# Row normalisation of 1024 x 4096: both stores issued by GpSimd, and the last scale of the first tile on VectorE alone

## The chip, the cores and the metric

The kernel runs on one core of a Trainium2 chip. Four of its engines matter here: VectorE and ScalarE compute, Sync and GpSimd issue transfers. The bytes are moved by 16 DMA engines, which take their work from queues; a transfer goes into the queue of the engine that issued it. The time is device microseconds of one execution; a figure quoted is a median of several. All runs here were in the fast state: the granted clock was 1.0 everywhere, and the executions of most kernels agree within 0.3%. "Span" is the time from the first to the last instruction in the trace; the timed figure is some 1.8 us longer for every kernel here, so what changes in the time is inside the span. One execution of each kernel was profiled, so each figure below that comes from a trace is of one execution.

## The reference

```python
batch, dim = 1024, 4096                       # x: float32
norm = np.sqrt(np.sum(x ** 2, axis=-1, keepdims=True) + eps)
return x / norm
```

So 16.78 MB are read and 16.78 MB are written, and each element is touched twice in between: once to square it, once to scale it.

## The kernel before

The 1024 rows are two tiles of 128 partitions x 4 rows x 4096. Both loads are issued at once by Sync. Each tile is squared (three rows on ScalarE, one on VectorE), scaled in place on VectorE, and stored in one transfer of 8.39 MB. Each tile has a buffer of its own, so no load waits for a store.

The lines on which the change rests, shortened (the whole kernel follows below):

```python
def scale(self, r):                            # VectorE, whole row
    nc.vector.tensor_scalar_mul(out=x[:, r], in0=x[:, r], scalar1=rstd[:, r:r+1])

def scale_by_both(self, r):                    # 7/8 on ScalarE, 1/8 on VectorE
    cut = 7 * D // 8
    nc.scalar.activation(out=x[:, r, :cut], in_=x[:, r, :cut], func=Copy, scale=rstd)
    nc.vector.tensor_scalar_mul(out=x[:, r, cut:], in0=x[:, r, cut:], scalar1=rstd)

for i, g in enumerate(groups):
    ...                                        # squares, norms, scales of rows 0, 1, 3
    g.square_act(2); g.norm(2)
    if i < n_tiles - 1:
        g.scale_by_both(2)                     # last scale of the first tile
    else:
        g.scale(2)
    store = nc.sync.dma_start(out=out_t[i], in_=g.flat())
gpsimd_waits_for_last_store(nc, store.ins)
```

The last line rewrites the program's teardown. That consists of two barriers of all engines (points at which each waits for the others), with drains ahead of them. A drain is an instruction at which an engine waits for its own earlier work: VectorE's took 2.39 us in the kernel before, beside its last scale of 2.35 us. Before the rewriting Sync waits for the last store. The rewriting lets only GpSimd wait for it, at the last step of the second barrier, so that everything else of both barriers happens while store 2 still moves.

## Time and profile before

| | before |
|---|---|
| median | 81.8 us |
| span of the profiled execution | 80.2 us |
| 16 DMA engines busy | 97.4% of the span |
| store 1 issued, load 2's data ends | 38.99 us; 40.27 to 41.05 us on the 16 engines |
| store 2 issued, store 1's data ends | 56.76 us; 59.79 to 60.37 us |
| last packet ends, span ends | 79.69 us, 80.20 us |

The busy share and the times of issue come from the views that the prediction shows. The ends of packets come from the records of single DMA packets in the trace: a packet here is one partition's 64 KiB, each of the 16 engines moves 32 of them one after the other, and nearly all take 2.418 us. To read a joint of two transfers one can take a stretch of the trace around it and divide busy time by bytes. In the stretch from 40.2 to 45.0 us, that is where load 2 gives way to store 1, the kernel before has (columns: stretch, length, busy DVE, ACT, POOL, clock, DMA share, GB/s):

```profile
40.20:45.00 4.80, 3.60 (x1) 3.60 (x2) 0.00 (x0) 1.00 1.01 437
79.70:80.20 0.50, 0.00 (x0) 0.00 (x0) 0.00 (x0) 1.00 0.00 0
```

437 GB/s for 4.8 us are 2.1 MB, two packets on each of the 16 engines, and a share of 1.01 says that the two together took 1.01 x 4.8 = 4.85 us, 2.42 us each. A share well over 1 in such a row means that packets which started in the stretch took longer than their usual time, if the stretch cuts no packets (a row in part 5 has 1.08 for that reason alone); so the readings below are checked against the packet records. Nor does a share of 1 rule out idle time: by the records, 5 of the 16 engines stood idle for 0.19 to 0.24 us between load 2 and store 1 here. They weren't the last to end, so it cost nothing. The second row is the tail after the last packet.

### The profile page before, as it was taken

Reading aid. Unit: us, or ns where it says so; the run is one execution under the profiler, and the core shown is the slowest. Engines: PE = TensorE matmul, PEld = TensorE weight load, DVE = VectorE, ACT = ScalarE, POOL = GpSimd, SP = SyncE. Lnnn points to the kernel's source line nnn. Section 1 sums busy time; section 2 is a strip of 40 time slices with the busy share of each in tenths; the row PEclk is TensorE's granted clock in tenths of the full one; section 3 lists DMA queues with packets and bytes.
Section 4 is the critical chain, followed back from the end, with each engine's and each line's share of the span. In section 5 each row is a group of like instructions: output and inputs, shape, how many; then the busy total and the mean of one; then the engine's idle time right before and its main releaser. Section 6 shows DMA issues by size and latency. Waiting matters only on the chain.

```text
span 80.2 us, 93 instructions
## 1 busy us (share of the span) xinstructions
DVE 26.7 (33%) x21; ACT 29.7 (37%) x23; POOL 0.2 (0%) x4
## 2 busy tenths in 40 slices
DVE  0000000000099599960039995999200000000000
ACT  6000000000099999989439999950000000000000
POOL 0000000000000000000000000000000000000000
DMA  9099996699996699996699990999991999992990
GB/s 490 33 523 523 523 490 294 261 523 523 523 490 261 294 523 523 523 490 261 294 523 523 523 490 33 523 523 523 523 458 65 523 523 523 523 425 98 523 523 0
DMA packets 576, 33.55 MB, mean 418 GB/s; under 512 B 64, under 2 KB 64, under 8 KB 64
## 3 DMA queue, kind: packets, MB, share of 16 engines
q1 hardware_dynamic: 576, 33.55, 97.4%
HBM read 16.78 MB, written 16.78 MB: 418 GB/s over the span
## 4 chain that ended last, share of the span: by engine, by line
DMA 51%; ACT 10%; DVE 9%; issue 0%
DMA xt<-in_x_dram 51%; ACT sq_act L33 9%; DVE xt L64 9%; ACT rstd L53 1%; DVE rstd L59 0%
## 5 line engine op out<-in xcount | busy, mean ns | idle before, releaser
L33 ACT ACTIVATE sq_act<-xt 128x4096 f32<-128x4096 f32 x6 | 21.7, 3609 | 22.4 <-DMA xt<-in_x_dram 22.4
L42 DVE SCALAR_TENSOR_TENSOR sq_dve<-xt 128x4096 f32<-128x4096 f32 x2 | 8.9, 4426 | 26.4 <-DMA xt<-in_x_dram 26.4
L64 DVE TENSOR_SCALAR xt<-xt,rstd 128x4096 f32<-128x4096 f32 x7 | 16.5, 2353 | 0.2
L72 ACT ACTIVATE xt<-xt,rstd 128x3584 f32<-128x3584 f32 x1 | 3.3, 3283 | 0.2 <-DVE rstd L59 0.2
L53 ACT ACTIVATE rstd<-ssq,eps_t 128x1 f32<-128x1 f32 x8 | 2.1, 290 | 0.1
L59 DVE RECIPROCAL rstd<-rstd 128x1 f32<-128x1 f32 x8 | 1.3, 160 | 2.5 <-ACT rstd L53 2.5
L33 ACT ACT_TABLE_LOAD x1 | 1.3, 1283 | 0.8 <-PEq L258 0.8
L53 ACT ACT_TABLE_LOAD x1 | 1.3, 1283 | 0.0
L33 ACT ACTIVATION_READ_ACCUMULATOR sq_act<-xt 128x1 f32 x6 | 1.1, 187 | 0.0
L78 DVE TENSOR_SCALAR xt<-xt,rstd 128x512 f32<-128x512 f32 x1 | 0.5, 487 | 0.0
L211 DVE MEMSET eps_t<- 128x1 f32 x1 | 0.1, 59 | 0.9 <-PEq L258 0.9
L42 DVE DVE_READ_ACCUMULATOR sq_dve<-xt 128x1 f32 x2 | 0.2, 83 | 0.0
L258 POOL MEMSET const-uint8-127<- 128x1 uint8 x1 | 0.1, 103 | 0.0
L258 POOL MEMSET const-bfloat16-1.0<- 128x1 bf16 x1 | 0.1, 102 | 0.0
L258 POOL MEMSET const-float32-0.0<- 128x1 f32 x1 | 0.1, 99 | 0.2 <-issue 0.2
L258 POOL MEMSET const-float32-1.0<- 128x1 f32 x1 | 0.1, 99 | 0.0
## 6 DMA issues: line engine op xcount, KB each, us to landing
xt<-in_x_dram SPq DMA_DIRECT2D x2, 31.3
out_dram<-xt SPq DMA_DIRECT2D x2, 22.5
```

The source lines that it names most:

```text
L33: self.nc.scalar.activation(out=sq_a, in_=self.x[:, r], func=ACT_F.Square, accum_out=self.ssq[:, r : r + 1],)
L42: self.nc.vector.scalar_tensor_tensor(out=sq_v, in0=self.x[:, r], scalar=1.0, in1=self.x[:, r], op0=ALU.mult, op1=ALU.mult, accum_out=self ...
L53: self.nc.scalar.activation(out=self.rstd[:, r : r + n], in_=self.ssq[:, r : r + n], func=ACT_F.Sqrt, bias=self.eps_t,)
L59: self.nc.vector.reciprocal(out=self.rstd[:, r : r + n], in_=self.rstd[:, r : r + n])
L64: self.nc.vector.tensor_scalar_mul(out=self.x[:, r], in0=self.x[:, r], scalar1=self.rstd[:, r : r + 1])
L72: self.nc.scalar.activation(out=self.x[:, r, :cut], in_=self.x[:, r, :cut], func=ACT_F.Copy, scale=rstd,)
L78: self.nc.vector.tensor_scalar_mul(out=self.x[:, r, cut:], in0=self.x[:, r, cut:], scalar1=rstd)
L211: nc.vector.memset(eps_t, eps)
L258: nc = _bacc.Bacc("TRN2", target_bir_lowering=False, num_devices=1)
```

## The change

Its intent, as far as the diff tells: GpSimd, idle until the end, takes the stores from Sync, and the first tile's last scale becomes shorter (one VectorE operation instead of two side by side of which ScalarE's is the longer). As GpSimd's queue is now used by the stores, its reset in the teardown goes behind the last landing.

```diff
-        if i < n_tiles - 1:
-            g.scale_by_both(2)
-        else:
-            g.scale(2)
-        store = nc.sync.dma_start(out=out_t[i], in_=g.flat())
+        g.scale(2)
+        store = nc.gpsimd.dma_start(out=out_t[i], in_=g.flat())
...                                            # teardown
-        tail.insert(taking, reset)
...
-        tail.insert(1 + where(semaphore)[-1], clear)
+        last = 1 + where(semaphore)[-1]
+        tail[last:last] = [reset, clear]
```

More of the change, by code (lines that the diff above doesn't have):

```diff
@@ L65, in scale @@
             out=self.x[:, r], in0=self.x[:, r], scalar1=self.rstd[:, r : r + 1]
-        )
-    def scale_by_both(self, r):
-        cut = 7 * self.D // 8
-        rstd = self.rstd[:, r : r + 1]
-        self.nc.scalar.activation(
-            out=self.x[:, r, :cut],
-            in_=self.x[:, r, :cut],
-            func=ACT_F.Copy,
-            scale=rstd,
-        )
-        self.nc.vector.tensor_scalar_mul(
-            out=self.x[:, r, cut:], in0=self.x[:, r, cut:], scalar1=rstd
         )
```

## The prediction

> **What bounds the kernel now.** I read the page first: the DMA rows of the slices, the queue line, the chain that ended last, and the DMA issues.
>
> ```profile
> DMA  9099996699996699996699990999991999992990
> GB/s 490 33 523 523 523 490 294 261 523 523 523 490 261 294 523 523 523 490 261 294 523 523 523 490 33 523 523 523 523 458 65 523 523 523 523 425 98 523 523 0
> ...
> q1 hardware_dynamic: 576, 33.55, 97.4%
> ...
> DMA 51%; ACT 10%; DVE 9%; issue 0%
> ...
> out_dram<-xt SPq DMA_DIRECT2D x2, 22.5
> ```
>
> The reader is to see that the 16 DMA engines are busy for 97.4% of the span: 0.974 x 80.2 = 78.1 us. The dips in the slice rows come from counting whole packets at one moment, not from gaps. The work is 33.55 MB in four transfers of 8.39 MB (load 1, load 2, store 1, store 2), each 128 rows of 64 KiB, so 512 large packets, 32 for each engine, and 78.1 / 32 = 2.44 us for one. The single packet records say the same: 2.418 us for nearly all, only the first of each engine takes some 3.15 us. Nothing else is near the bound: ACT is busy 37%, DVE 33%. The chain stops at the last scale, because the rest of the span is the last store.
>
> Next, the timeline around the two stores, in two windows (start in us, duration in us, engine, line, operation).
>
> ```profile
> 35.68 3.28 ACT L72 ACTIVATE xt<-xt,rstd 128x3584 f32<-128x3584 f32 x1 [0.23 <-DVE rstd L59]
> 35.68 0.49 DVE L78 TENSOR_SCALAR xt<-xt,rstd 128x512 f32<-128x512 f32 x1
> 38.99 0.35 SPq L240 DMA_DIRECT2D out_dram<-xt  x1
> ...
> 54.38 2.35 DVE L64 TENSOR_SCALAR xt<-xt,rstd 128x4096 f32<-128x4096 f32 x1
> 56.76 0.34 SPq L240 DMA_DIRECT2D out_dram<-xt  x1
> ```
>
> and the busy share in chosen stretches (DVE, ACT, POOL, clock, DMA share, GB/s):
>
> ```profile
> 37.80:40.50 2.70, 0.00 (x0) 1.17 (x1) 0.00 (x0) 1.00 1.01 437
> 40.50:59.80 19.30, 14.23 (x10) 11.88 (x10) 0.00 (x0) 1.00 1.00 431
> 59.80:79.70 19.90, 0.00 (x0) 0.00 (x0) 0.00 (x0) 1.00 0.97 418
> ```
>
> The reader is to see that both stores are issued well before the engines could start on them. Store 1 is issued at 38.99, but in the packet records the last load-2 packets end between 40.47 and 41.05 on the 16 engines, and each engine's first store packet starts at the same moment. So store 1 has 1.5 us of slack on the earliest engine. Store 2 is issued at 56.76, and store 1's packets end between 59.79 and 60.37, so it has 3.0 us. The DMA share is 1.0 across both joints (0.97 at the end, where engines finish one by one up to 79.69). The stream is gapless from about 1.0 us (first packet) to 79.7 us.
>
> Then the end of the program: the teardown instructions.
>
> ```profile
> L272 POOLq EVENT_SEMAPHORE  x4: 17/17/17, 57.3 to 80.1; - x4
> ...
> L272 POOLq DRAIN  x3: 34/41/64, 0.7 to 57.5; - x3
> ...
> L272 POOLq EVENT_SEMAPHORE_RANGE_CLEAR  x1: 71/71/71, 80.1 to 80.1; - x1
> ```
>
> The last packet ends at 79.69, GpSimd sees the landing at 80.05, clears at 80.13 and the span ends at 80.20: 0.5 us of tail. The timed median is 81.8, so 1.6 us lie outside the profiled span.
>
> **What the Trainium skill says.** "DMA: Bandwidth & Descriptors", section "Issuing engines are not separate DMA queues": transfers issued by Sync, Scalar or GpSimd run on the same 16 DMA engines, and another issuer saves only issue time. Here issue time is 0.34 us in a stream of 78 us and hidden; the trace has only one issuer and can't confirm the rest. The same page, section "Queues, rings and completion order": each DMA engine takes turns between the queues that have work, a whole packet at a time. The trace has one queue only, so it is silent; but it gives the packet, 2.418 us, which decides how much a second queue could hurt. The same page, "Specifications": first byte about 1 us for a transfer issued by GpSimd, about 0.6 us from Sync. In the trace load 1 is issued at 0.00 and its first packet starts at 1.02 (with a cold start); no run shows the GpSimd figure yet. "SBUF — State Buffer", in its note on the "DVE blocks DMA" trap: GpSimd cannot write descriptors while VectorE runs an operation in a two-port mode, and fp32 scaling is of that kind. The trace agrees that the scale runs fast: 4096 elements in 2353 ns, against 4426 ns for the squaring with two inputs, so nearly two elements at a time.
>
> **The change part by part.**
>
> 1. The last scale of tile 1. Removed: ACT 3.28 us and DVE 0.49 us side by side, both from 35.68. Added: one whole VectorE scale, 2.35 us by the seven of its kind (2353 to 2355 ns). Ready at 35.68 + 2.35 = 38.03 in place of 38.96: 0.93 us earlier. DVE has 5.2 us idle there (from 36.17 until load 2 lands at 41.40), so the extra 1.87 us on it cost nothing; ACT loses 3.28 us of work that delayed nothing. Gain on the bound: 0, because the DMA engines have no free time to use an earlier store.
>
> 2. The issue of store 1 by GpSimd, at about 38.07 (38.03 plus the 0.03 us seen between such steps). With a first byte after an estimated 1.0 us (the Trainium skill's figure, the page above) its packets are there at about 39.1. Slack until the first engine is out of load work at 40.47: 1.4 us, nearly as before (1.5 us). Gap: 0.
>    It is a second queue now, so it no longer stands behind load 2 by order. But each engine's last load-2 packet started between 37.85 and 38.62, before 39.1. With turns of whole packets nothing is left of load 2 to be overtaken: it lands at 41.4 as before, and tile 2 runs as before to 56.75.
>
> 3. The issue of store 2 by GpSimd at 56.76 plus about 1.0 us: 57.8, in the same queue behind store 1, which ends at 59.8 to 60.4. Slack 2.0 us instead of 3.0. Gap: 0.
>
> 4. Descriptors against VectorE. Store 1 waits for the very scale that could block it, and the next VectorE work starts at 41.40; 3.3 us are free for the 128 rows. Behind store 2 there is no VectorE work at all. Cost: 0.
>
> 5. The teardown. GpSimd's reset drain, 34 to 64 ns here at 57.5 and hidden behind store 2, moves behind the last landing, between the release and the clear. Added on the path: 0.04 to 0.07 us if it stays as short, 0.18 us if it takes as long as GpSimd's first drain after its four memsets (181 ns at 0.30 us in the trace). I take 0.1 us. The landing of a GpSimd store may be reported a little later too; I add another 0.1 us as a guess.
>
> Sum: 0 + 0 + 0 + 0 + 0.2 = 0.2 us. 81.8 + 0.2 = 82.0 us.
>
> **The rivals.**
>
> A. Store 1 gets in ahead of load 2. If GpSimd's packets arrive before 38.62, some engines put one store packet in front of their last load packet, and load 2 lands up to 2.4 us later, near 43.8. If an engine shares two queues more finely than by packets, the rest of load 2 (some 1.4 to 1.9 us after 39.1) takes twice as long, landing near 43.0. Tile 2 then ends at 58.4 to 59.2 and store 2's packets are there at 59.4 to 60.2, around the end of store 1 (59.8 to 60.4). The total of bytes is the same, so this eats the slack first and costs at most 0.4 us: 82.0 to 82.4. For it: the store is ready 0.93 us sooner. Against it: the GpSimd start is thought to be slower. It would show in the trace as a later start of tile 2 and yet no loss.
>
> B. GpSimd is slow to start. If it needs over 2.4 us from the scale to the first packet, the DMA engines run dry between 40.5 and the first packet, and every us more is a us of time; a start of 4 us would give 83.6. Store 2 has 3.0 us before the same happens. For it: nothing in this trace has GpSimd issuing a transfer. Against it: the skill's figure is less than half of the slack.
>
> C. GpSimd's stores stream more slowly, because rows are cut smaller, or some DMA engines also serve the descriptors' memory. Each percent on two stores of 19.3 us is 0.39 us; 4% would be 1.6 us and make it slower by 2%. Against it: rows of 64 KiB leave few descriptors, 8 for each engine and store.
>
> D. A gain. Only the 2.1 us of the span in which the stream isn't running (80.2 - 78.1) could shrink, and the change doesn't touch the start. Reading and writing at once for a short while might go above 433 GB/s, but the packet time is 2.418 us for loads and stores alike, so the engine is the limit and not the direction. Under 0.3 us: 81.5 at best.
>
> **Range and chances.** The expected time is 82.0. The lower end, 81.6, is rival D with a free teardown. The upper end, 83.0, is rival B with a start near 3.3 us, or C at 2.5%, or A with an expensive teardown. Faster by 2% means below 80.2, which the stream of 78.1 us plus its 2.1 us of start and tail plus the 1.6 us outside forbids: 0.01. Slower by 2% means above 83.4, so 1.6 us lost, which needs B or C in strong form or a heavier teardown with GpSimd's queue in use: 0.12. The same: 0.87.
>
> **What would show it.** Right: two queues in the profile, with 16.78 MB each; DMA share near 97%; tile 2's first squares at 41.4; the store issues on GpSimd at 38.07 and 56.76, and no DMA stretch below full share around 40.5 or 60; the span 80.2 to 80.5. Wrong on step 2: tile 2 starts at 43 or later. Wrong on rival B: a hole in the DMA stream just after 41. Wrong on rival C: store packets longer than 2.418 us, or more of them than 128 for a store. Wrong on step 5: over 0.3 us between the last packet's landing and the end of the span. If the median moves by more than 1.6 us and the stream still looks full inside the span, the cost lies in what runs outside of it, which I can't see here.

## The result, and the profile after

| | before | after |
|---|---|---|
| median (5 runs each) | 81.83 us | 84.02 us |
| ratio, with 95% interval | | 1.0266 (1.0251 to 1.0281) |
| span of the profiled execution | 80.20 us | 82.28 us |
| first packet of store 1 on an engine, median | 2.42 us | 3.76 us |
| last packet ends | 79.69 us | 80.89 us |
| from there to the end of the span | 0.51 us | 1.39 us |

Ratios are the mean time of one kernel's fast runs over that of the other's of the same rounds, so not quite the ratio of the medians. The changed kernel is slower by 2.2 us. In the two traces 2.08 us of it are in two places: 1.20 us in the stream of transfers, 0.88 us behind it. (The profiled execution of the kernel before was one of its longer ones; in later calls its spans were 79.8 to 80.3 us.)

The parts of the changed kernel's page that answer to those of before:

```profile
DMA  9299999849999994999909994999999399999830
...
q0 software_dynamic: 288, 16.78, 48.7%
q1 hardware_dynamic: 288, 16.78, 47.9%
...
out_dram<-xt POOLq DMA_DIRECT2D x2, 24.0
```

There are two queues now, with half of the bytes each. The loads' queue has 0.479 x 82.3 = 39.4 us of busy time on each engine; the stores' queue has 0.487 x 82.3 = 40.1 us for 16 packets, where 16 x 2.418 would be 38.7. So the stores cost 1.4 us more than they should. The loads' surplus of 0.7 us is their first packets at the start, which the kernel before has too.

The timeline at the places that the prediction looked at:

```profile
35.63 2.35 DVE L64 TENSOR_SCALAR xt<-xt,rstd 128x4096 f32<-128x4096 f32 x1
38.29 0.67 POOL L223 DMA_DIRECT2D out_dram<-xt  x1 [37.85 <-DVE xt L64]
41.34 3.62 ACT L33 ACTIVATE sq_act<-xt 128x4096 f32<-128x4096 f32 x1 [5.95 <-DMA xt<-in_x_dram]
...
56.98 0.53 POOL L223 DMA_DIRECT2D out_dram<-xt  x1 [18.02 <-DVE xt L64]
```

Store 1 is issued 0.70 us sooner, load 2 lands at 41.34 (41.40 before), tile 2 starts and ends as before. Nothing is late up to here. But the stretch around the joint, and the one behind the last packet:

```profile
40.20:45.00 4.80, 3.66 (x1) 3.66 (x2) 0.00 (x0) 1.00 1.29 437
80.90:82.30 1.40, 0.00 (x0) 0.00 (x0) 0.00 (x0) 1.00 0.00 0
```

The same 437 GB/s now took a share of 1.29 instead of 1.01: 0.28 x 4.8 = 1.34 us more on each engine. The packet records say which: the first store packet of every engine starts within 3 ns of the end of its load work and takes 3.64 to 3.98 us; every later packet takes 2.418 us. The stream has no hole; one packet of each engine is 1.35 us too long. As the loads were a little better aligned in this execution, the end moves by 1.20 us.

The teardown (all instructions of it stand on one line of the kernel; the three numbers are the shortest, median and longest in ns, then first and last start in us):

```profile
L255 POOLq EVENT_SEMAPHORE  x4: 17/17/17, 81.5 to 82.0; - x4
...
L255 POOLq DRAIN  x3: 41/76/24479, 57.0 to 82.1; - x3
...
L255 POOLq EVENT_SEMAPHORE_RANGE_CLEAR  x1: 96/96/96, 82.2 to 82.2; - x1
```

In the kernel before GpSimd's barrier steps began at 57.3 us; here the first is at 81.5. The reason is one drain of 24,479 ns, from 56.95 to 81.43 us: it ends 0.13 us after the last report that store 2 has landed (81.30). So both barriers, which ran under store 2 before, now come after it, and the trick of the teardown is void.

### The profile page after: what moved, and what is told of

Same layout as the page of the kernel before. It is cut to its first block, busy times and chain, and to the rows that moved or that the text cites. A ratio compares the mean times of both kernels' runs of the same rounds, so it can differ in the third digit from the quotient of the medians.

```text
span 82.3 us, 92 instructions
## 1 busy us (share of the span) xinstructions
DVE 28.6 (35%) x21; ACT 26.4 (32%) x22; POOL 1.4 (2%) x6
## 4 chain that ended last, share of the span: by engine, by line
DMA 49%; issue 19%; POOLq 1%
DMA xt<-in_x_dram 49%; POOLq L255 1%; POOLq L223 0%
## 5 line engine op out<-in xcount | busy, mean ns | idle before, releaser
L64 DVE TENSOR_SCALAR xt<-xt,rstd 128x4096 f32<-128x4096 f32 x8 | 18.8, 2353 | 0.3
L42 DVE SCALAR_TENSOR_TENSOR sq_dve<-xt 128x4096 f32<-128x4096 f32 x2 | 8.8, 4425 | 24.5 <-DMA xt<-in_x_dram 24.5
L223 POOL DMA_DIRECT2D out_dram<-xt x2 | 1.2, 598 | 55.9 <-DVE xt L64 55.9
```

The costliest lines, as they stand in the source:

```text
L42: self.nc.vector.scalar_tensor_tensor(out=sq_v, in0=self.x[:, r], scalar=1.0, in1=self.x[:, r], op0=ALU.mult, op1=ALU.mult, accum_out=self ...
L64: self.nc.vector.tensor_scalar_mul(out=self.x[:, r], in0=self.x[:, r], scalar1=self.rstd[:, r : r + 1])
L223: store = nc.gpsimd.dma_start(out=out_t[i], in_=g.flat())
```

## The experiments

Two explanations to be tested. Main theory: the loss is the sum of a slow joint in the stream (from store 1 in a second queue, while load 2 still moves) and of the drain. Rivals: GpSimd's queue is new to the DMA engines and the first packets are slow for that; its descriptors (the entries that tell a DMA engine what to move) are slow; changing queues costs as such; or the shift of the scale matters by itself. In the table, "joint" is the median duration of an engine's last load packet, of its first packet of store 1 and of store 2 (2.42 is the normal), and "tail" runs from the last packet to the end of the span. "Issued" is when store 1 was. Each ratio is to the kernel before on the same chip.

| run | store 1 / store 2 by | issued, us | joint: load, store 1, store 2 | tail, us | time, us | ratio |
|---|---|---|---|---|---|---|
| before | Sync / Sync | 38.99 | 2.43, 2.42, 2.42 | 0.51 | 81.83 | |
| after | GpSimd / GpSimd | 38.29 | 2.42, **3.76**, 2.42 | 1.39 | 84.02 | 1.0266 |
| scale_only | Sync / Sync | 37.86 | **2.74**, 2.42, 2.42 | 0.52 | 82.43 | 1.006 |
| issue_only | GpSimd / GpSimd | 39.11 | 2.42, 2.50, 2.42 | 1.34 | 83.09 | 1.0146 |
| act_queue | ScalarE / ScalarE | 37.91 | **2.73**, **3.11**, 2.42 | 0.68 | 82.87 | 1.0125 |
| warm | GpSimd / GpSimd | 38.40 | 2.42, **3.80**, 2.42 | 1.47 | 84.37 | 1.0298 |
| late_drain | GpSimd / GpSimd | 38.21 | 2.43, **3.78**, 2.42 | 1.02 | 83.79 | 1.0223 |
| delay | GpSimd / GpSimd | 38.82 | 2.42, 2.57, 2.42 | 1.35 | 83.10 | 1.0162 |
| act_late | ScalarE / ScalarE | 38.80 | 2.42, **3.24**, 2.42 | 0.68 | 82.71 | 1.0096 |
| late_both | GpSimd / GpSimd | 39.01 | 2.42, 2.51, 2.42 | 0.97 | 82.72 | 1.0097 |
| first_late | GpSimd / Sync | 39.13 | 2.42, 2.56, 2.42 | 0.73 | 82.49 | 1.0071 |
| last_late | Sync / GpSimd | 38.67 | 2.43, 2.42, **3.75** | 1.36 | 83.93 | 1.025 |
| tiny | Sync / Sync | 38.81 | 2.42, 2.42, 2.42 | 0.61 | 81.96 | 1.0015 |
| early | GpSimd / GpSimd | 35.05 | **3.49**, 2.42, 2.46 | 1.34 | 84.46 | 1.0316 |
| early_sp | Sync / Sync | 34.73 | **3.65**, 2.42, 2.42 | 0.52 | 83.18 | 1.0164 |
| sp_act | Sync / ScalarE | 38.78 | 2.43, 2.42, 2.42 | 0.54 | 81.85 | 1.0001 |
| act_sp | ScalarE / Sync | 38.86 | 2.42, **3.23**, 2.42 | 0.58 | 82.74 | 1.0106 |

One more run, three, has half packets and is told below. Medians are of 4 runs, of early, early_sp and three of 2.

### 1. Each part alone

scale_only: the kernel before with the VectorE scale.

```diff
-        if i < n_tiles - 1:
-            g.scale_by_both(2)
-        else:
-            g.scale(2)
+        g.scale(2)
```

> Only the scale of the first tile goes to VectorE alone; both stores stay on Sync. If the transfers bound it at every moment, the earlier store 1 (ready 0.93 us sooner) buys nothing: 81.8 us, within 0.1 of before, and all store packets at 2.42 us. If the scale were a part of the loss, some of the 2.2 us would show here.

Measured: 82.43 us, ratio 1.006 (1.0044 to 1.0075). A miss of the expectation: the earlier store costs 0.5 us although no engine and no queue changed. Its last load packets took 2.74 us instead of 2.42. The stretch from 37.8 to 45.0 us, first in scale_only and then in the kernel before (columns as above):

```profile
37.80:45.00 7.20, 3.46 (x2) 3.42 (x1) 0.00 (x0) 1.00 1.05 437
```

```profile
37.80:45.00 7.20, 3.60 (x1) 4.77 (x3) 0.00 (x0) 1.00 1.01 437
```

The share of 1.05 against 1.01 is 0.04 x 7.2 = 0.3 us. So the slow split scale of the kernel before, which makes store 1 wait, is worth something: the store then comes as load 2 ends, and not while it moves.

issue_only: the changed kernel with the split scale kept.

```diff
-        g.scale(2)
+        if i < n_tiles - 1:
+            g.scale_by_both(2)
+        else:
+            g.scale(2)
         store = nc.gpsimd.dma_start(out=out_t[i], in_=g.flat())
```

> Only the issuer changes; the scale stays split over ScalarE and VectorE. If the whole loss is the issuer's: 84.0 us, with the first store packets of each engine near 3.7 us and 1.4 us between the last packet and the end of the span. As store 1 is then ready 0.9 us later, a start of GpSimd of over about 1.3 us would add a hole in the stream in front of store 1 and make it up to 0.5 us slower than the changed kernel.

Measured: 83.09 us, ratio 1.0146. A miss again: only half of the loss, and first store packets of 2.46 to 2.65 us. The same issuer, 0.8 us later, and the slow packets are gone:

```profile
40.20:45.00 4.80, 3.74 (x1) 3.71 (x2) 0.00 (x0) 1.00 1.03 437
```

The first packet starts at 40.64 us, 1.53 us after the issue, and each of the 16 engines stood idle for 0.18 to 0.24 us at the joint. What stays of the loss is that and the tail of 1.34 us. The parts give 0.5 + 1.15 = 1.65 us against 2.2 together, so they are not independent: the early store costs 0.3 us in Sync's queue and 1.35 us in GpSimd's.

### 2. Who issues, and a queue that has been used

act_queue: the changed kernel with `nc.scalar.dma_start` for both stores.

> The changed kernel with both stores issued by ScalarE, so on a second hardware queue. If a queue's first packets are slow because the queue is new to the engines (cold), or because the engines change queues (switch): first store packets near 3.7 us and the time 1.2 us over before, 83.0, with the tail of before (0.5 us). If only the descriptors that GpSimd writes are slow: packets at 2.42 us and 81.8 us.

Measured: 82.87 us. Descriptors written by GpSimd aren't needed for a slow joint: in ScalarE's hardware queue the last load packets took 2.73 and the first store packets 3.11 us, 1.0 us in sum.

warm: a small load by GpSimd at the start, which nothing reads.

```diff
+    warm = scratch_pool.tile([P, 128], F32)
+    nc.gpsimd.dma_start(out=warm, in_=x_t[0][:, :128])
```

> The changed kernel plus one small load issued by GpSimd at the start, which nothing reads. If the cost is that of a cold queue, store 1's first packets fall to 2.42 us and the time to 82.8 us (only the longer tail is left). If it is the change from one queue to another, or GpSimd's own start per transfer, they stay near 3.7 us and the time at 84.0 us.

Measured: 84.37 us, first store packets 3.66 to 3.97 us. A queue that is new to the engines isn't the cause, at least not one that small packets would cure.

### 3. Is it the time of arrival?

delay: the changed kernel with one more VectorE operation, on which store 1 depends.

```diff
         g.scale(2)
+        if i == 0:
+            nc.vector.tensor_scalar_mul(out=g.x[:, 2, :1024], in0=g.x[:, 2, :1024], scalar1=1.0)
```

> The changed kernel with one more VectorE operation on which store 1 depends (times 1.0 on a quarter of the row, about 0.85 us), so that GpSimd issues it near 39.15 us as in the run with the scale on both engines, but without ScalarE. Timing theory (a store that reaches the DMA engines while load 2's last packets move costs them time): first store packets 2.5 us in place of 3.76, and 83.1 us. If it was ScalarE's part in the scale that made the difference: 84.0 us or over, packets 3.7 us.

Measured: 83.06, 83.10, 83.10 and 83.91 us. This is the clearest run. The profiled execution is the one of 83.91, and in it 15 of the 16 engines have first store packets of 2.46 to 2.65 us and one has 3.78. That one ended last, 0.9 us behind the next, and the time is that of the slowest engine; the three faster executions weren't traced, so that no engine paid in them is inferred from their time. The 15 stood idle for 0.19 to 0.23 us between load and store (their starts and ends paired in order of time); the slow one went on within 2 ns. So it is a race of each engine for itself: an engine that goes on to the store at once pays 1.35 us, one that has to wait for it pays that wait and 0.04 to 0.23 us on its packet. The view of the joint agrees, with 0.05 x 4.8 = 0.24 us on each engine in the mean (1.29 in the changed kernel):

```profile
40.20:45.00 4.80, 3.85 (x1) 3.82 (x3) 0.00 (x0) 1.00 1.05 437
```

Where the border lies is seen from the time between the issue of store 1 by GpSimd and the end of an engine's load work. Up to 1.79 us no engine paid (issue_only, late_both, first_late); from 1.92 us on all did (after, warm, late_drain); in delay, with 1.44 to 1.97 us, the one at 1.92 us paid and one at 1.97 us didn't. So it isn't the 1.53 us after which the first store packet starts in issue_only: by that (38.82 + 1.53 = 40.35), some 12 of delay's 16 engines would have paid. The waits don't look like an arrival at one moment either, as they are all near 0.2 us although the load work ended anywhere from 40.26 to 40.79 us. ScalarE's part in the scale plays no role.

act_late: both stores in ScalarE's queue, with the split scale.

> Both stores on ScalarE's queue, with the scale split over ScalarE and VectorE as in the kernel before, so store 1 is issued near 39.0 us. Timing theory: no loss in a second queue either if it comes as load 2 ends; last load and first store packets 2.42 to 2.5 us, 81.8 to 82.1 us. If changing queues costs by itself: first store packets over 3 us and 82.9 us as with the early store on that queue.

Measured: 82.71 us, first store packets 3.07 to 3.49 us. The expectation of the timing theory is missed at first sight. But ScalarE issues right behind its own part of the scale, at 38.80, and all its packets were there before the engines had finished (every gap at the joint is under 10 ns). So the run doesn't contradict the race; it shows that in ScalarE's queue losing it costs 0.8 us instead of 1.35. The reset moves behind the landing here as in the changed kernel, but GpSimd has no transfers, and the tail is 0.68 us (so in act_queue): 0.17 us over the kernel before is what the moved reset and a slightly later landing cost by themselves.

### 4. The drain

late_drain: GpSimd's two plain drains of the teardown go behind the landing as well.

```diff
+        plain = where(lambda i: i.engine == POOL and isinstance(i, mybir.InstDrain))
+        late = [tail[n] for n in plain]
+        for n in reversed(plain):
+            tail.pop(n)
         last = 1 + where(semaphore)[-1]
-        tail[last:last] = [reset, clear]
+        tail[last:last] = late + [reset, clear]
```

> The changed kernel, but GpSimd's two plain drains of the teardown come after the landing of store 2 instead of ahead of the two barriers. Theory D (the drain waits for the transfers that GpSimd issued, so both barriers come after the last landing, 1.4 us of tail in place of 0.5): the tail falls to some 0.6 us and the time to 83.2 us, with the slow first store packets left as they are (3.7 us). If the longer tail has another cause, for instance a later report of the landing, the time stays at 84.0 us.

Measured: 83.79 us, tail 1.02 us instead of 1.39. GpSimd's lines of the teardown:

```profile
L259 POOLq EVENT_SEMAPHORE  x4: 17/17/17, 56.9 to 81.4; - x4
...
L259 POOLq DRAIN  x3: 34/76/222, 81.5 to 81.8; - x3
```

The first barrier is back at 56.9 us, so the drain was what held it. But the gain is 0.37 us and not 0.8: a drain behind landed stores still takes 222 ns, and with the others and the clear 0.5 us remain in a row behind the landing.

late_both: the split scale and the late drains in one (the diffs of issue_only and late_drain).

> Both repairs in one: GpSimd issues both stores, the scale is split as before (store issued near 39.1 us), and the drains come after the landing. If the loss is the sum of early store 1 (about 1.0) and drain (about 0.85), this stands at 82.2 us, 0.3 over before: GpSimd's issue alone costs little. If there is a third cost of GpSimd's issue, it is over 82.6 us.

Measured: 82.72 us, ratio 1.0097, where 82.2 was expected. Joint 2.51 us, tail 0.97. What is left over the kernel before is the tail (0.46 us) and the short waits at the joint (0.15 to 0.38 us, from 79.84 us as the last packet's end against 79.46 to 79.69 in runs with Sync's stores at that time).

tiny: the kernel before plus a load of 4 bytes per partition by GpSimd at the start.

```diff
+    tiny = scratch_pool.tile([P, 1], F32)
+    nc.gpsimd.dma_start(out=tiny, in_=x_t[0][:, :1])
```

> The kernel before plus one load of 4 bytes per partition issued by GpSimd at the start, which nothing reads. It shows what the mere use of GpSimd's queue costs: 81.9 us, within 0.2 of before, if the costs are those of the stores; up to 0.5 us more if the teardown is longer as soon as that queue has been used.

Measured: 81.96 us, ratio 1.0015 (0.9993 to 1.0036). The mere use of GpSimd's queue costs nothing that can be told. Its drain waits here too, but for that small load:

```profile
L275 POOLq DRAIN  x3: 41/76/8615, 1.2 to 57.4; - x3
```

### 5. One store by GpSimd, one by Sync

first_late and last_late: issue_only with one of its stores given back to Sync.

```diff
-        store = nc.gpsimd.dma_start(out=out_t[i], in_=g.flat())
+        store = (nc.gpsimd if i == 0 else nc.sync).dma_start(...)     # first_late
+        store = (nc.sync if i == 0 else nc.gpsimd).dma_start(...)     # last_late
```

> GpSimd issues store 1 only, late as in the run with the scale on both engines; Sync issues store 2. GpSimd's transfer has then landed long before the end, so theory D says that its drain ends near 61 us and the tail is that of before, 0.5 us. If each change of queue with work waiting costs (switch theory), store 2's first packets take 3.1 to 3.8 us and the time is 82.9 us; if only a store coming up behind a load costs, they take 2.42 us and the time is 82.0 us.

> Sync issues store 1 as in the kernel before, GpSimd issues store 2. Theory D: the drain ends after store 2 and the tail is 1.4 us, so 0.85 us over before, 82.7 us, if a store behind a store in another queue costs nothing; with 0.7 to 1.35 us more, 83.4 to 84.0 us, if each change of queue with work waiting costs.

Measured: 82.49 and 83.93 us. In first_late the drain ends with store 1, long before the end:

```profile
L273 POOLq EVENT_SEMAPHORE  x4: 17/17/17, 61.2 to 80.4; - x4
...
L273 POOLq DRAIN  x3: 41/76/22014, 39.1 to 80.4; - x3
```

39.1 + 22.0 = 61.1 us, just after store 1's landing (61.03), and the tail is 0.73. The time is 0.5 us over the 82.0 expected: 0.2 us of tail, and the short waits at the joint as in late_both. Store 2's first packets, in Sync's queue behind GpSimd's, took 2.42 us: this change of queue is free. In last_late the order is the other way round, and store 2's first packets took 3.55 to 3.94 us on 13 of the 16 engines and 2.42 on three:

```profile
59.50:64.00 4.50, 0.00 (x0) 0.00 (x0) 0.00 (x0) 1.00 1.32 466
```

So for GpSimd's queue it needn't be a load that goes before: a store that waits there while Sync's queue finishes pays as well. Time 83.93 us, as much as the whole change, with one store of GpSimd.

sp_act and act_sp: the same with ScalarE in place of GpSimd, on the kernel before.

> The kernel before with store 2 on ScalarE's queue, store 1 on Sync's as before. Store 2 then waits in a second hardware queue behind store 1. If a waiting packet in any second queue that is new to the DMA engines costs (0.7 to 0.8 us for ScalarE's queue as seen behind a load): first packets of store 2 3.1 to 3.5 us, 82.6 us. If it costs only behind a load: 2.42 us and 81.9 us.

> The kernel before with store 1 on ScalarE's queue, store 2 on Sync's. Store 1 pays its 0.8 us as in the run with both on that queue. Store 2 changes back to a queue that has been in use: if the cost is that of a queue new to the engines, or of a change away from Sync's queue, store 2's first packets take 2.42 us and it stands at 82.7 us; if each change with work waiting costs, 3.1 us and 83.4 us.

Measured: 81.85 us (ratio 1.0001) and 82.74 us. In the matching stretch of sp_act, where store 2 waits in ScalarE's queue behind store 1 in Sync's, there is no loss (1.08 is also the share of the kernel before around its own joint of the stores, since the stretch cuts packets):

```profile
59.40:63.90 4.50, 0.00 (x0) 0.00 (x0) 0.00 (x0) 1.00 1.08 466
```

So ScalarE's queue, new and waiting, is free behind a store; behind a load it costs (act_sp: 3.23 us, as in act_late; one of its engines, idle for 0.24 us at the joint, took 2.46). The way back to Sync is free. sp_act ties with the kernel before; no version beat it.

### 6. Earlier still

early: the changed kernel without the scale of the first tile's row 2. Wrong result; the store can go 3.2 us sooner.

```diff
-        g.scale(2)
+        if i > 0:
+            g.scale(2)
```

> Wrong result on purpose: row 2 of the first tile isn't scaled, so GpSimd issues store 1 near 35.2 us, while each DMA engine still has a whole load-2 packet to start. With turns of whole packets (rival A of the prediction) load 2 lands up to 2.4 us later, near 43.8 us, and tile 2 starts there; the stream loses again some 1.2 us if the loss comes at each change of queue, more if at each of two changes. If load 2 lands at 41.4 us, a waiting second queue is served only when the first has nothing left.

Measured: 84.46 us. The extra time (1.07 us) is now in the last load packets, the first store packets are normal, and tile 2 starts late:

```profile
35.05 0.67 POOL L224 DMA_DIRECT2D out_dram<-xt  x1 [34.61 <-DVE xt L64]
...
44.75 3.62 ACT L33 ACTIVATE sq_act<-xt 128x4096 f32<-128x4096 f32 x1 [9.48 <-DMA xt<-in_x_dram]
```

The load's data was complete on every engine by 41.96 us, but the small packet with which an engine reports the landing came at 43.80 to 44.37 us, right after the first store packet of that engine. So the engines do take turns between the queues by whole packets, and what was overtaken is not load data but the report. The turn came later than rival A had it: each engine's last load packet, which started at 37.8 to 38.5 us, still went ahead of the store issued at 35.05. Tile 2 lost 3.4 us; its slack took most of it, as rival A of the prediction said it would, and the engines stood idle for 0.4 to 0.8 us ahead of store 2.

early_sp: the same with Sync as issuer (scale_only without that scale).

> Wrong result on purpose: row 2 of the first tile isn't scaled, so Sync issues store 1 near 35.2 us in the same queue as load 2. In one queue the load's landing can't be passed: load 2 lands near 41.4 us, and the loss is that seen with the early store on Sync, 0.3 to 0.5 us: 82.4 us. If the loss grows with how early the store is, it is 83 us or more.

Measured: 83.18 us, where 82.4 was expected. In one queue the report can't be overtaken, but the last load packets took 3.65 us, 1.2 us too long. So the cost of a store that comes while the load moves grows in Sync's own queue with how early it is: nothing at 38.99, 0.33 us per engine at 37.86, 1.23 us at 34.73. (No run delays scale_only's store as delay does, so that it is the time and not the changed scale rests on these three points.)

three: issue_only, with the first tile's store cut in two halves, one issued by GpSimd and one by Sync.

```diff
+        if i == 0:
+            half = R * D // 2
+            nc.gpsimd.dma_start(out=out_t[i][:, :half], in_=g.flat()[:, :half])
+            nc.sync.dma_start(out=out_t[i][:, half:], in_=g.flat()[:, half:])
+        else:
             store = nc.gpsimd.dma_start(out=out_t[i], in_=g.flat())
```

> Store 1 goes half through GpSimd's and half through Sync's queue, both issued near 39.1 us, store 2 through GpSimd's. GpSimd's queue has then moved full-size packets a few us before store 2. If its slow first packets are those of a queue new to the engines, store 2's are fast, 2.42 us; if they come with each change from Sync's queue to GpSimd's with a packet waiting, they are near 3.7 us again. Packets of store 1 that take turns between the two queues show whether each turn costs.

Measured: 84.99 us, ratio 1.0386. GpSimd's half was ready and issued at 35.09 us, so it met the load as in early (last load packets 3.33 us; the load's report at 42.5 to 42.9). Then the two queues took turns, packet by packet, and each half packet of 32 KiB took 1.213 us, half of 2.418: turns cost nothing. Then store 2, in GpSimd's queue that had moved large packets a moment ago, behind Sync's half, had first packets of 3.65 us in the median (2.42 on four engines). So it is neither a new queue nor the change of queues as such.

### What stays open

Shown: a store that waits when the engine's load work ends makes one packet of each engine longer, by 1.35 us in GpSimd's queue, 0.8 to 1.0 us in ScalarE's and 0 to 1.2 us in Sync's own, by its time of arrival; if it comes just after, there is only a short wait. In GpSimd's queue the same happens behind a store of Sync's. Not shown: what in the DMA engine takes that time. The records give start and duration of a packet, not what its reading and its writing side wait for. Nor is it clear what sets the border between waiting and not: behind Sync's store, engines of three paid from 1.7 us after the issue on, and those that escaped were the last three to finish store 1 in last_late (60.00 to 60.05 us) and, in three, the last three and one more.

## Why the prediction was wrong

**The bound and the slack (right for the bound, the slack misread).** The stream of packets sets the end; store 1 and store 2 were in time, no hole opened at 40.5 or 60, load 2 landed at 41.34, tile 2 ended as before. GpSimd's issue to first packet was 1.1 us on idle engines (store 2 of early: 60.39 to 61.50) and 1.53 us in issue_only, within the 2.4 us of rival B's limit; the first is near the 1.0 us that was estimated. GpSimd took 0.31 us from the end of the scale (37.98) to the issue (38.29), where 0.03 was assumed; it opened no hole. Two readings of the kernel before were off. The 40.47 us at which the first engine was said to run out of load work is the start of the first store packet: load work ended at 40.27, and five engines stood idle for about 0.2 us there, so the stream wasn't gapless and Sync's store wasn't 1.5 us early, but just in time. And the 1.6 us outside the span are 1.84, as the profiled execution took 82.04 us.

**Step 1, the earlier scale: "Gain on the bound: 0" (wrong in sign).** The argument was that a full stream has no use for an earlier store. It has none, but the earlier store disturbs it: scale_only lost 0.5 us, with last load packets of 2.74 us.

**Step 2, "Gap: 0" and so cost 0 (the step that failed most).** No gap, and yet 1.35 us per engine. I counted packets at 2.418 us whatever stood beside them, and took "the same bytes" for "the same time". Rival A moved in that direction, but it let the cost fall on load 2's landing and be absorbed by slack, "at most 0.4 us". In the changed kernel it fell on the store's own first packets, where no slack is. Rival C's sign, store packets over 2.418 us, was the one to see, but for one packet of 16 on each engine, not at a few per cent for all.

**Step 3 (right).** Store 2 behind store 1 in the same queue: 2.42 us packets. last_late shows that this isn't owed to GpSimd's good start but to its queue being the one at work.

**Step 4 (nothing seen against it).** VectorE had no part in it: delay has a VectorE operation more, and the joint is better.

**Step 5, the teardown: 0.1 us for the reset and 0.1 us for the landing (a term was missing: 0.88 us).** The two terms were good: where the reset is moved and GpSimd has no transfers (act_queue, act_late), the tail grows by 0.17 us. What was missed, some 0.7 us, stands in the same list of instructions: another drain of GpSimd ahead of the first barrier, 41 ns in the kernel before. I asked only what the moved instruction costs, not what the drains that stay would wait for, now that GpSimd has transfers of its own. The drain held both barriers until the landing.

**The sum.** 0.2 us predicted, 2.2 us measured; 1.20 of it in the joint, 0.88 in the teardown. The stated signs of error named both places, if not the causes ("store packets longer than 2.418 us", "over 0.3 us between the last packet's landing and the end of the span"), but at 0.12 the chance for slower was too low, as two independent surprises were each given little.

## What to carry to other kernels

A full DMA stream isn't a neutral belt: look at the joints between transfers, and at the time at which the next one arrives. A store that arrives just as the load ends may be better than an earlier one, and a deliberately slow operation ahead of it may be there for that. Before giving an idle engine a transfer, follow that engine to the end of the program: GpSimd's drain waited for what it had issued (24.5 us here), and all that stands behind the drain moves with it.

## What the Trainium skill lacked or had wrong

- "DMA: Bandwidth & Descriptors", "Issuing engines are not separate DMA queues": that another issuer only saves issue time holds for the bandwidth (turns between two queues cost nothing here, 1.213 us for half packets), but it lacks that a packet which waits in GpSimd's queue while another queue finishes took 3.76 us instead of 2.42, and 3.24 us in ScalarE's queue behind a load.
- The same page, "Queues, rings and completion order": turns of whole packets are as the runs show them, but it doesn't say that a whole packet of another queue can go between a transfer's last data and its report: load 2's reports left 2.4 us after its data (41.4 to 42.0 against 43.8 to 44.4 us in early).
- No page has that GpSimd's drain waits for the transfers that GpSimd issued: 24.5 us behind store 2, 22.0 us behind store 1, 8.6 us behind a load of 4 bytes per partition.
